# Sums of the tokens added up in DRAM beside S5, a turn without raw copies, and plain products ahead of the sums' products in a hybrid decoder block

## The chip, the cores and the metric

The kernel runs on one core of one Trainium2 chip. The metric is the device time of one execution in microseconds (us). TensorE is called PE, its weight loads PEld, VectorE DVE, ScalarE ACT, GpSimd POOL, and SyncE, which issues most of the loads, SP.

## The reference, cut to what matters

One layer of a decoder block on 1024 tokens of width 1024: a token-mixing sub-layer, a cross-attention into 256 memory rows, and a SwiGLU layer, all in float32. The change lies in the mixing sub-layer:

```python
h = rms_norm(x, g_mix_pre)
z = h @ w_in                                   # 1024 x 4608
z_gm, z_s5, z_ga, z_gb = split(z)              # 2048 | 512 | 1024 | 1024 columns
u, v = split(gelu(z_gm))                       # 2 x 1024
y_gm = u * (W_s (layer_norm(v)) + b_s)         # causal, inside chunks of 128 tokens, 8 groups
y_s5 = s5(z_s5)                                # diagonal complex SSM over all tokens, gelu
y_s5 = y_s5 * sigmoid(y_s5 @ w_glu)
merged = sigmoid(z_ga) * (y_gm @ w_br_gm) + sigmoid(z_gb) * (y_s5 @ w_br_s5)
x = x + rms_norm(merged @ w_mix_out, g_mix_post)
```

## The kernel before, in words

**Products.** Every float32 factor is split into two float32r parts, hi and lo = value - hi (`put`, L527: ACT copies hi, DVE subtracts), and a product is three float32r matmuls (`mm3`, L521). The normed input h stands turned (channels on partitions) in `hT`, eight pairs of 128 x 1024; its first 512 columns are the first half of the tokens (h0), the others the second (h1). `self.slot()` takes one of 38 SBUF tiles of 128 x 1024, `self.bank()` one of the 8 PSUM banks; a new holder waits until the old one's last use.

**Order.** All engines' programs are written out by hand, in one order. The main line writes PE's products; after every six or so it calls `sub()` (L67), a step, which lets each queued generator (`bg`, with a delay in steps) write its next piece and then splits the next weights (`pump`, `split`, L98, with L103 on ACT and L104 on DVE; the weights' loads L94 are on SP, three ahead). `yield n` in a generator means n steps. Each engine works through its own instructions strictly in this order and stops where a semaphore isn't there yet; the DMAs that SP, ACT and POOL issue stand in those queues too.

**Start.** `start` (L650) projects the memory to keys and values and meanwhile turns x: `xgen` squares, scales and, in `h_turn` (L766), transposes four token tiles per k into one bank, from which ACT (L533) and DVE (L140) make the pair in `hT`. For 12 of the 16 banks ACT then also copies the scaled raw value (L783), negated for some, and POOL stores it to `td` in DRAM (L784). Then the S5 parameters are loaded (L203 to L209) and turned (L220).

**S5 and gates.** `s5_in`, `gates` (16 gate blocks, whose results wait in DRAM) and two `u_block`s are the main line, while `s5_gen` (L720) runs eight S5 blocks: `s5_c` rotates and scans on DVE, `s5_d` (L498, with L506 to L508 on PE) gives y, which is turned (L755, copied by ACT at L756) and stored to `yd`.

**u and v.** The remaining u columns (in pairs m = 2, 4, 6) and all v columns use Winograd's form of a 2 x 2 block product: seven products instead of eight, on sums of token blocks (T1 to T4) and sums of weight blocks. `h_split` (L787) makes the token sums behind S5: SP loads the raw parts into slots, POOL adds with accumulating DMAs (L791) from `td` and `hT`, and each sum is split by `put` or by L824; T3, T2 and T4 come each from the sum before, by further adds. `w_ops` (L900) does the weights: `uv_sides` (L926) loads them and names POOL's sums (L137), ACT casts (L912), DVE subtracts; up to eight such operands stand ahead. `u_pairs` (L991) takes them in the order 11, 21, T1, T2, 22, T3 per pair, T4 with the next pair. `v_phase` (L1121) runs 11, T1, T2, 22, T3, 21 and T4 into the banks X (four) and Y (four), with gelus, the layer norm `ln`, and `wturn` (L1193), which transposes W_s (L1198, copied by ACT at L1199), behind T4.

**Gate and gating.** `s5_out` (L1035) makes S5's gate (L1051) and then projects S5's branch (`bs`, evicted by DVE), and from its second weight block on `gm_gen` (L1234) multiplies v with W_s per group and half: PE, two DVE operations (L1257, L1259), and a `put`. `merge` (L1266) needs all eight groups.

```python
        for m in (2, 4, 6):
            prod(b, "11", True)
            prod(e, "21", True)
            prod(d, "T1", True)
            prod(b, "T2", False)
            prod(d, "22", False)
            prod(b, "T3", False)      # T4 with the next pair
```

Of the kernel before, what the change touches and what calls it, by code (L numbers as in the profile page):

```python
# [9 lines left out]
F = mybir.dt.float32  # L10
# [26 lines left out]
class Builder:  # L37
# [565 lines left out]
    def consts(self):  # L603
        nc, i = self.nc, self.ins
        self.ident = self.cp.tile([P, P], F, name="ident", tag="ident")
        make_identity(nc, self.ident)
        g = self.cp.tile([40, P], F, name="grow", tag="grow")
        for j, n in enumerate(("g_mix_pre", "g_ca_pre", "g_ffn_pre", "g_mem", "gm_ln_g")):
            nc.sync.dma_start(g[8 * j:8 * j + 8], i[n][0].rearrange("(k p) -> k p", p=P))
        self.gc = self.cp.tile([P, 48], F, name="gc", tag="gc")  # L610
        ps = self.bank()
        nc.tensor.transpose(ps[:, 0:40], g, self.ident[0:40, 0:40])
        nc.vector.tensor_copy(self.gc[:, 0:40], ps[:, 0:40])
        self.ts(self.gc[:, 40:48], self.gc[:, 0:8], -1.0, ALU.mult)
# [35 lines left out]
    def start(self):  # L650
# [27 lines left out]
        def xgen():  # L678
            for half in range(2):
# [10 lines left out]
                yield from self.h_turn(xs[4 * half:4 * half + 4], half)  # L690
# [4 lines left out]
            self.bg(self.s5_gen(), 5)  # L695
        self.bg(xgen())
# [23 lines left out]
    def s5_gen(self):  # L720
# [28 lines left out]
        for q in range(4):  # L749
            y, t = self.yq.pop(q), self.slot()  # L750
            for jh in range(2):
                ps = self.bank()
                for j in range(4):
                    o = (4 * jh + j) * 128
                    self.nc.tensor.transpose(ps[:, j * 128:j * 128 + 128], y[:, o:o + 128], self.ident)  # L755
                self.nc.scalar.copy(t.rearrange("p (c j) -> p j c", j=8)[:, 4 * jh:4 * jh + 4],  # L756
                                    ps.rearrange("p (j c) -> p j c", j=4))
                yield 2
# [3 lines left out]
            y = t = None  # L762
        yield 1
        self.nc.scalar.dma_start(*late)

    def h_turn(self, xs, half):  # L766

        nc = self.nc
        if not half:
            self.td = self.dr.tile([12, P, 512], F, name="td", tag="td")  # L770
        o = slice(half * 512, half * 512 + 512)
        r = None
        for k in range(8):
            ps = self.bank()
            for t, x in enumerate(xs):
                nc.tensor.transpose(ps[:, t * 128:t * 128 + 128], x[:, k * 128:k * 128 + 128], self.ident)
            self.put_scaled(tuple(z[:, o] for z in self.hT[k]), ps, self.gc[:, k:k + 1])
            if not half or k < 4:
                if k % 2 == 0:
                    r = self.slot()  # L780
                c = slice(k % 2 * 512, k % 2 * 512 + 512)
                n = 40 if half or k >= 4 else 0
                nc.scalar.mul(r[:, c], ps, self.gc[:, n + k:n + k + 1])  # L783
                nc.gpsimd.dma_start(self.td[8 * half + k], r[:, c])  # L784
            yield 1

    def h_split(self):  # L787

        nc = self.nc
        h0, h1 = slice(0, 512), slice(512, 1024)  # L790
        acc = lambda dst, src: nc.gpsimd.dma_start(dst, src, accum_op=ALU.add)  # L791
        raw = [self.slot() for _ in range(4)]
        for k in range(4):
            nc.sync.dma_start(raw[k][:, h0], self.td[8 + k])
            nc.sync.dma_start(raw[k][:, h1], self.td[8 + k])
        for k in range(4):
            acc(raw[k][:, h0], self.td[k])
        for z in range(2):
            for k in range(4):
                acc(raw[k][:, h1], self.hT[k + 4][z][:, h1].bitcast(F))  # L800
            yield 1

        def t1():
            for k in range(4):
                self.put(tuple(x[:, h1] for x in self.hT[k]), raw[k][:, h0])
                if k % 2:
                    yield 1
            self.sides.add("T1")
        early = self.plain
        if early:  # L810
            yield from t1()
        for k in range(4):
            self.put(self.fx("T3", k, True), raw[k][:, h1])
            acc(raw[k][:, h1], self.td[k])
            if k % 2:
                yield 1
        self.sides.add("T3")
        if not early:
            while not self.plain:
                yield 1  # L820
            yield from t1()
        for k in range(4):
            dst, x = self.fx("T2", k, True), raw[k][:, h1]
            nc.scalar.mul(dst[0], x, -1.0)  # L824
            self.stt(dst[1], x, -1.0, dst[0].bitcast(F), ALU.mult, ALU.subtract)
            acc(raw[k][:, h1], self.td[4 + k])
            if k % 2:
                yield 1
        self.sides.add("T2")
        for k in range(4):  # L830
            self.put(self.fx("T4", k, True), raw[k][:, h1])
            if k % 2:
                yield 1
        self.sides.add("T4")
# [91 lines left out]
    def uv_sides(self):  # L926
# [5 lines left out]
        def raw(m):  # L932
            g, u = self.wr.tile([P, 1024], F, name="wr", tag="wr"), self.slot()
            for t, c in ((g, m * 128), (u, m * 128 + 128)):
                ld(t.rearrange("p (k c) -> p k c", k=8), wi[:, c:c + 128].rearrange("(k p) c -> p k c", p=P))
            return g, u
        nxt, old = raw(2), None
        for m in (2, 4, 6):
            g, u = nxt
            nxt = raw(m + 2) if m < 6 else None  # L940
            d, s = self.tmp(), self.tmp()
            yield g[:, h0], ()
            yield g[:, h1], ()
            if old is not None:
                yield old, ()
            yield d, ((d, u[:, h0], u[:, h1], A),)
# [3 lines left out]
            old, g, u = u[:, h1], None, None  # L950
# [6 lines left out]
        r = {}  # L957
        for k in range(2):
            r[k] = row(k)
        for k in (2, 3, 4, 5, 6, 7):  # L960
            r[k] = row(k)
        a, b = [r[k] for k in range(4)], [r[k + 4] for k in range(4)]
        r.clear()
        for k in range(4):
            yield a[k][:, h0], ()
        yield old, ()
# [24 lines left out]
    def u_pairs(self):  # L991
# [14 lines left out]
        fin = None  # L1006
        for m in (2, 4, 6):
            b, d, e = self.bank(), self.bank(), self.bank()
            u, v = self.slot(), self.slot()
# [4 lines left out]
            if fin:  # L1014
                fin()
# [16 lines left out]
            b = d = e = u = v = None  # L1032
        return fin

    def s5_out(self):  # L1035
# [28 lines left out]
        lg(1)  # L1064
        late = []
# [16 lines left out]
        self.bg(self.gm_gen(), 1)  # L1082
# [38 lines left out]
    def v_phase(self, fin):  # L1121
# [71 lines left out]
        def wturn():  # L1193
            for h in (h0, h1):
# [5 lines left out]
                yield 2  # L1200
            for h in (h0, h1):
# [5 lines left out]
                yield 1  # L1207
# [16 lines left out]
        Y = None  # L1224
        run(X, "T4", False)
# [6 lines left out]
        self.bg(wturn(), 3)  # L1232

    def gm_gen(self):  # L1234
# [11 lines left out]
        for g in range(8):  # L1246
# [3 lines left out]
            for half in range(2):  # L1250
# [10 lines left out]
                yield 1 + half  # L1261
# [608 lines left out]
    def go(self, out):  # L1870
        i = self.ins
        self.make_plan()
        self.s5s, self.yq, self.zok, self.xok, self.vok, self.yok, self.plain, self.vhalf = {}, {}, False, False, False, False, False, False
# [7 lines left out]
        self.bg(self.w_ops(self.uv_sides()), 1)  # L1881
# [57 lines left out]
```

## Time and profile before

| | us |
|---|---|
| median of 3 runs | 1700.07 |
| lowest, highest | 1698.69, 1701.0 |
| the profiled execution's own time | 1700.28 |
| its span, first to last instruction | 1698.6 |
| PE busy in the span | 1642.0 |
| DVE, ACT, POOL busy | 1148.9, 688.9, 69.8 |
| granted PE clock, mean | 0.986 |

The granted clock is PE's, as a share of full speed; its two levels are 1.2 and 2.4 GHz, so 0.5 means the lower one. PE's matmuls are pipelined, so durations of neighbours overlap and the distance between starts tells the rate. An idle time stands in brackets behind an instruction, with the instruction or transfer that ended it.

### The profile page before, as it was taken

The page shows a single profiled execution, that of the slowest core. Times are in us where ns is not written, and L with a number is a line of the kernel's source. Part 1 is how long each engine was busy: PE and PEld are TensorE (multiplying, and loading weights), DVE is VectorE, ACT ScalarE, POOL GpSimd, SP SyncE. Part 2 cuts the span into 40 slices and gives each one's busy share as a digit, 9 for nine tenths or more (in the row PEclk, how much of TensorE's full clock was granted, in tenths as well). Part 3 has the DMA queues.
Part 4 walks back from the last instruction along what each step waited for, and adds up shares of the span by engine and source line. Part 5 has one row for each costly group of instructions (what it writes and reads, how often), then busy time and mean ns, then how long its engine had stood idle before and what let it go on. Part 6 is the DMA issues. An engine that isn't in the chain of part 4 may idle for free.

```text
span 1698.6 us, 20955 instructions
## 1 busy us (share of the span) xinstructions
PE 1642.0 (97%) x7788; PEld 1369.9 (81%) x7788; DVE 1148.9 (68%) x2046; ACT 688.9 (41%) x1200; POOL 69.8 (4%) x73
## 2 busy tenths in 40 slices
PE   7899999997999899999999999999999999999998
PEld 7688878875888787888888888888888888888886
DVE  5569788975335476437765567796777778676778
ACT  6622222225446522124554347763333233244454
POOL 0100000034230000000000000000000000000000
PEclk9899999997999999999999999999999999999999
DMA  8532313167440356345431334674544546363634
GB/s 291 183 98 75 95 66 94 58 170 156 149 161 18 122 208 223 124 149 186 149 112 50 126 127 132 208 226 155 183 141 153 186 137 203 134 234 128 226 111 168
DMA packets 206069, 251.13 MB, mean 148 GB/s; under 512 B 14312, under 2 KB 138256, under 8 KB 205968
## 3 DMA queue, kind: packets, MB, share of 16 engines
q1 hardware_dynamic: 175056, 179.14, 33.1%
q10 hardware_dynamic: 26496, 60.18, 9.5%
q0 software_dynamic: 4416, 10.49, 2.6%
q8 instruction: 61, 1.00, 0.2%
q14 instruction: 40, 0.33, 0.1%
HBM read 180.16 MB, written 65.80 MB: 145 GB/s over the span
## 4 chain that ended last, share of the span: by engine, by line
PE 56%; DVE 3%; ACT 1%; issue 1%; DMA 1%; DVEq 0%; ACTq 0%
PE ps L519 55%; DVE act L134 1%; DVE act L140 1%; DMA wr<-actd 1%; DVE ws L134 1%; ACT jk L575 0%; PE ps L1443 0%; PE ps L1397 0%; PE ps L587 0%; DVE ws L104 0%; DVE act L530 0%; DVE st L140 0%; ACT act L529 0%; ACT act L1385 0%; ACT ws L103 0%
## 5 line engine op out<-in xcount | busy, mean ns | idle before, releaser
L519 PE MATMUL ps<-act,ws 128*128 128x512 f32 (+1 forms) x4212 | 975.5, 389 | 15.1 <-ACT act L824 4.2
L519 PEld LDWEIGHTS ps<-act,ws 128*128 128x128 f32 x4212 | 776.4, 189 | 174.6 <-ACT act L824 5.8
L519 PE MATMUL ps<-ws,act 128*128 128x512 f32 x1392 | 339.2, 400 | 4.2 <-ACT ws L103 2.5
L519 PEld LDWEIGHTS ps<-ws,act 128*128 128x128 f32 x1392 | 273.3, 209 | 53.1 <-ACT ws L103 3.4
L134 DVE TENSOR_TENSOR act<-act 128x512 f32<-128x512 f32 (+6 forms) x521 | 290.8, 587 | 15.6 <-ACT act L1051 8.4
L519 PE MATMUL ps<-ws 128*128 128x512 f32 x852 | 193.3, 389 | 0.0
L104 DVE TENSOR_TENSOR ws<-wr,ws 128x1024 fp32r<-128x1024 f32 x100 | 122.0, 1223 | 100.2 <-ACT ws L103 100.2
L519 PEld LDWEIGHTS ps<-ws 128*128 128x128 f32 x852 | 159.9, 188 | 33.2
L134 DVE TENSOR_TENSOR act<-ps,act 128x512 f32<-128x512 f32 x201 | 135.9, 685 | 34.8 <-PE ps L519 32.0
L134 DVE TENSOR_TENSOR ws<-tm,ws 128x512 fp32r<-128x512 f32 x108 | 81.4, 755 | 82.7 <-ACT ws L1522 58.5
L134 DVE TENSOR_TENSOR ws<-act,ws 128x512 fp32r<-128x512 f32 x107 | 73.9, 691 | 89.1 <-ACT ws L1729 51.8
L134 DVE TENSOR_TENSOR ws<-wr,ws 128x512 fp32r<-128x512 f32 x130 | 92.3, 711 | 50.3 <-ACT ws L912 35.2
L1522 ACT CAST ws<-tm 128x512 fp32r<-128x512 f32 x88 | 54.8, 622 | 168.3 <-PE ps L519 115.2
L103 ACT CAST ws<-wr 128x1024 fp32r<-128x1024 f32 x100 | 104.5, 1047 | 43.7 <-PE ps L519 32.5
L529 ACT CAST act<-act 128x512 fp32r<-128x512 f32 (+1 forms) x92 | 57.6, 639 | 124.7 <-DVE act L134 117.2
L530 DVE TENSOR_TENSOR act<-act 128x512 fp32r<-128x512 f32 (+1 forms) x92 | 64.7, 713 | 53.4 <-ACT act L529 47.2
L519 PE MATMUL ps<-act 128*128 128x256 f32 (+2 forms) x504 | 87.3, 319 | 4.2 <-ACT act L1199 4.0
L519 PEld LDWEIGHTS ps<-act 128*128 128x128 f32 x504 | 75.0, 191 | 14.4 <-ACT act L1199 4.9
L1729 ACT CAST ws<-act 128x512 fp32r<-128x512 f32 x71 | 44.2, 622 | 89.6 <-PE ps L519 48.3
L530 DVE TENSOR_TENSOR act<-ps,act 128x512 fp32r<-128x512 f32 x48 | 32.5, 688 | 39.7 <-ACT act L529 39.7
L877 ACT ACTIVATE act<-ps 128x512 f32<-128x512 f32 x32 | 19.2, 601 | 77.6 <-PE ps L519 50.8
L1806 POOL DMA_DIRECT2D out_dram<-act x4 | 2.2, 554 | 1170.5 <-DVE act L134 1170.5
(164 smaller groups left out, 1080.1 us busy)
## 6 DMA issues: line engine op xcount, KB each, us to landing
wr<-in_ffn_w_gu_dram SPq DMA_DIRECT2D x39, 512.0 KB, 4.1
actd<-act ACTq DMA_DIRECT2D x77, 256.0 KB, 2.1
wr<-actd SPq DMA_DIRECT2D x38, 512.0 KB, 3.6
wr<-in_w_in_dram SPq DMA_DIRECT2D x28, 512.0 KB, 3.9
act<-in_ffn_w_gu_dram SPq DMA_DIRECT2D x22, 512.0 KB, 5.1
act<-in_ffn_w_down_dram SPq DMA_DIRECT2D x44, 256.0 KB, 4.4
pd<-act ACTq DMA_DIRECT2D x17, 512.0 KB, 3.7
act<-pd SPq DMA_DIRECT2D x34, 256.0 KB, 4.3
```

Source lines behind the costliest of these rows:

```text
L103: self.nc.scalar.copy(hi, t)
L104: self.nc.vector.tensor_tensor(out=lo, in0=t, in1=hi.bitcast(F), op=ALU.subtract)
L134: self.nc.vector.tensor_tensor(out=out, in0=a, in1=b, op=op)
L140: self.nc.vector.scalar_tensor_tensor(out=out, in0=a, scalar=s, in1=b, op0=op0, op1=op1)
L519: self.nc.tensor.matmul(ps, a, b, start=start, stop=stop, skip_group_check=more)
L529: self.nc.scalar.copy(dst[0], src)
L530: self.nc.vector.tensor_tensor(out=dst[1], in0=src, in1=dst[0].bitcast(F), op=ALU.subtract)
L877: nc.scalar.activation(out=g[:, half * 512:half * 512 + 512], in_=ps, func=AF.Sigmoid)
L1522: self.nc.scalar.copy(t[:, 0:512], now)
L1729: nc.scalar.copy(w[:, h[0]], src)
L1806: nc.gpsimd.dma_start(out[t * P:t * P + P], os_[t])
```

## The change

x's turn becomes the plain `turn` and makes only the pairs in `hT`. A new generator `h_sums` starts eight steps after x is turned and makes T1 to T4 in a DRAM tile `td` of 20 parts of 128 x 512: ACT negates the two parts of h that are subtracted, and POOL stores, copies and adds with DMAs from `hT` and from `td` itself. `h_split` loads each finished sum on SP and splits it, T2 ahead of T1 while the u blocks still read `hT`, T3 and T4 not before y is turned. y's turn is copied by DVE, one step apart instead of two, and S5's last product comes one step later. The weights' operands start five steps later and in a new order, since the plain products (11 and 21) of pairs 2 and 4 now come first and those of pair 6 behind pair 4; fewer rows of the v weights are loaded at once. `wturn` starts ahead of T4's run, with longer distances, and `gm_gen` three steps into the first block of S5's branch, two steps between halves.

```diff
                 yield 4
-                yield from self.h_turn(xs[4 * half:4 * half + 4], half)
+                yield from self.turn(xs[4 * half:4 * half + 4], 0, hs(half))
                 for t in range(4):
                     xs[4 * half + t] = None
             self.xok = True
             self.s5_load()
             self.bg(self.s5_gen(), 5)
+            self.bg(self.h_sums(), 8)
...
             if b < 7:
                 yield from self.s5_b(b + 1)
             else:
-                yield 3
+                yield 4
             yield from self.s5_d(b)
...
-                self.nc.scalar.copy(t.rearrange("p (c j) -> p j c", j=8)[:, 4 * jh:4 * jh + 4],
-                                    ps.rearrange("p (j c) -> p j c", j=4))
-                yield 2
+                self.nc.vector.tensor_copy(t.rearrange("p (c j) -> p j c", j=8)[:, 4 * jh:4 * jh + 4],
+                                           ps.rearrange("p (j c) -> p j c", j=4))
+                yield 1
...
+        self.yturned = True
...
-    def h_turn(self, xs, half):
...
+    def h_sums(self):
...
+        self.td = self.dr.tile([20, P, 512], F, name="td", tag="td")
+        part = lambda j, k: self.td[4 * j + k]
+        add = lambda dst, src: nc.gpsimd.dma_start(dst, src, accum_op=ALU.add, max_dma_last_dim=512)
+        self.T = {"T1": 0, "T3": 1, "T2": 2, "T4": 3}
+        for j, (o, h) in ((0, (0, h1)), (4, (4, h0))):
+            for k in range(4):
+                n = self.slot()
+                for c, z in ((h0, 0), (h1, 1)):
+                    nc.scalar.mul(n[:, c], self.hT[k + o][z][:, h].bitcast(F), -1.0)
+                nc.gpsimd.dma_start(part(j, k), n[:, h0])
+                yield 2
+                add(part(j, k), n[:, h1])
+                yield 2
+                n = None
+        for k in range(4):
+            nc.gpsimd.dma_start(part(1, k), part(0, k))
+        yield 4
+        for j, o, h in ((1, 4, h1), (0, 0, h0)):
+            for z in range(2):
+                for k in range(4):
+                    add(part(j, k), self.hT[k + o][z][:, h].bitcast(F))
+                    yield 1
+                yield 4
+        for k in range(4):
+            nc.gpsimd.dma_start(part(2, k), part(1, k))
+            yield 1
+        yield 4
+        for z in range(2):
+            for k in range(4):
+                add(part(2, k), self.hT[k][z][:, h0].bitcast(F))
+                yield 1
+            yield 4
+        for k in range(4):
+            nc.gpsimd.dma_start(part(3, k), part(2, k))
+            yield 1
+        yield 4
+        for k in range(4):
+            add(part(3, k), part(4, k))
+            yield 1
...
     def h_split(self):
...
+        def ld(n):
+            r = []
             for k in range(4):
+                if k % 2 == 0:
+                    r.append(self.slot())
+                nc.sync.dma_start(r[-1][:, k % 2 * 512:k % 2 * 512 + 512], self.td[4 * self.T[n] + k])
+            return r
+        raw = {n: ld(n) for n in ("T1", "T2")}
+        todo = ["T1", "T2", "T3", "T4"]
+        while todo:
+            n = todo[todo[0] == "T1" and not self.plain and len(todo) > 1]
+            while n == "T1" and not self.plain:
+                yield 1
+            todo.remove(n)
+            if n not in raw:
+                raw[n] = ld(n)
+            r = raw.pop(n)
+            while n in ("T3", "T4") and not self.yturned:
+                yield 1
+            for k in range(4):
+                x = r[k // 2][:, k % 2 * 512:k % 2 * 512 + 512]
+                if n == "T1":
+                    self.put(tuple(z[:, 512:1024] for z in self.hT[k]), x)
+                elif n == "T2":
+                    dst = self.fx(n, k, True)
+                    nc.scalar.mul(dst[0], x, -1.0)
+                    self.stt(dst[1], x, -1.0, dst[0].bitcast(F), ALU.mult, ALU.subtract)
+                else:
+                    self.put(self.fx(n, k, True), x)
                 if k % 2:
                     yield 1
...
+            self.sides.add(n)
...
+        gs = [raw(m) for m in (2, 4, 6)]
+        us = [raw(3)]
+        for g in gs[:2]:
             yield g[:, h0], ()
             yield g[:, h1], ()
...
+            if j == 1:
+                yield gs[2][:, h0], ()
+                yield gs[2][:, h1], ()
...
+        a, b = [row(k) for k in range(4)], []
         for k in range(4):
             yield a[k][:, h0], ()
+            b.append(row(k + 4))
...
+        plain(2)
+        plain(4)
+        fin = lambda: None
+        for m in (2, 4, 6):
+            b, d = bank.pop(m), self.bank()
+            u, v = out.pop(m), self.slot()
             prod(d, "T1", True)
             nc.scalar.copy(v[:, h1], d)
+            fin()
             prod(b, "T2", False)
             nc.scalar.copy(u[:, h1], b)
+            self.later()
             prod(d, "22", False)
...
+            if m == 4:
+                plain(6)
...
         lg(1)
+        self.bg(self.gm_gen(), 3)
         late = []
         w = self.get(("bs", 0))
...
-        self.bg(self.gm_gen(), 1)
...
                 nc.scalar.copy(self.wt[:, h], ps)
-                yield 2
+                yield 4
...
                 self.tt(self.bb[:, h], ps, self.bb[:, h], ALU.add)
-                yield 1
+                yield 2
...
         Y = None
+        self.bg(wturn(), 2)
         run(X, "T4", False)
...
         self.bg(ln(0))
-        self.bg(wturn(), 3)
...
                 self.put(tuple(s[:, o] for s in y), u[:, o])
-                yield 1 + half
+                yield 2
...
-        self.bg(self.w_ops(self.uv_sides()), 1)
+        self.bg(self.w_ops(self.uv_sides()), 6)
```

## Rows read from the trace of the kernel before

**Rows 1.** Stretches: PE, PEld, DVE, ACT, POOL busy (instructions), granted clock, DMA share, GB/s.
```profile
43.13:111.23 68.10, 58.20 (x231) 48.35 (x229) 41.46 (x132) 30.70 (x46) 6.71 (x11) 0.90 0.50 159
361.29:363.89 2.60, 2.60 (x26) 2.60 (x24) 0.00 (x0) 0.00 (x0) 0.00 (x0) 1.00 0.29 65
378.49:431.15 52.66, 39.23 (x156) 30.13 (x155) 27.64 (x41) 26.67 (x40) 21.63 (x22) 0.77 0.70 139
82.00:355.00 273.00, 267.18 (x1397) 229.34 (x1398) 225.95 (x569) 64.44 (x118) 3.97 (x4) 0.99 0.29 87
546.19:578.69 32.50, 28.00 (x127) 22.49 (x126) 14.20 (x30) 25.03 (x44) 0.00 (x0) 0.95 0.16 51
```
**Rows 2.** The same view for the products of L519 alone (PE, PEld).
```profile
43.13:111.23 68.10, 55.16 (x192) 44.17 (x192) 0.90 0.50 159
378.49:431.15 52.66, 31.78 (x100) 20.91 (x100) 0.77 0.70 139
```
**Rows 3.** Timeline of PE, start: start, duration, instruction, count, [idle before, what ended it].
```profile
52.70 0.50 PE L519 MATMUL ps<-ws,act 128*128 128x512 f32 x1 [1.64 <-ACT ws L103]
53.96 10.20 PE L519 MATMUL ps<-ws,act 128*128 128x512 f32 x29 [0.76 <-DVE ws L104]
65.68 0.30 PE L776 MATMUL ps<-ident,act 128*128 128x128 f32 x1 [1.52 <-DVE act L144]
...
92.73 0.22 PE L220 MATMUL ps<-ident,act 32*128 32x32 f32 x1 [3.25 <-DMA act<-in_s_lam_re_dram]
...
93.35 17.95 PE L519 MATMUL ps<-ws,act 128*128 128x512 f32 x66
```
**Rows 4.** Timeline of ACT in the first turn: a raw copy and a split of weights.
```profile
48.94 0.69 ACT L783 ACTIVATE act<-ps,gc 128x512 f32<-128x512 f32 x1 [1.36 <-DVE act L140]
...
51.61 1.03 ACT L103 CAST ws<-wr 128x1024 fp32r<-128x1024 f32 x1
```
**Rows 5.** Timeline of PE from S5's last block to the first u pair.
```profile
378.49 0.38 PE L506 MATMUL ps<-act 128*128 128x128 f32 x2
...
388.09 4.36 PE L519 MATMUL ps<-act,ws 128*128 128x512 f32 x18
...
406.32 0.79 PE L519 MATMUL ps<-act,ws 128*128 128x512 f32 x1 [3.83 <-ACT act L824]
...
423.80 2.93 PE L519 MATMUL ps<-act,ws 128*128 128x512 f32 x9 [3.20 <-ACT act L1019]
```
**Rows 6.** Timeline of ACT, DVE and POOL in the same stretch.
```profile
365.12 0.62 ACT L912 CAST ws<-wr 128x512 fp32r<-128x512 f32 x1 [7.94 <-DMA act<-act]
...
371.39 4.87 DVE L134 TENSOR_TENSOR act<-act 128x512 f32<-128x512 f32 x3
...
376.84 4.92 POOL L791 DMA_DIRECT2D act<-act  x4
...
390.09 0.87 POOL L791 DMA_DIRECT2D act<-act  x1 [0.40 <-DMA act<-act]
...
420.71 1.08 ACT L756 COPY act<-ps 128x512 f32<-128x512 f32 x1 [5.13 <-DVE act L530]
```
**Rows 7.** Timeline of PE and DVE from v's products to S5's gate.
```profile
480.91 65.44 PE L519 MATMUL ps<-ws,act 128*128 128x512 f32 x288
540.67 2.48 DVE L134 TENSOR_TENSOR act<-ps,act 128x512 f32<-128x512 f32 x4
...
560.85 1.16 PE L519 MATMUL ps<-act 128*128 128x128 f32 x8 [4.02 <-ACT act L1199]
```
**Rows 8.** DVE by line, 590 to 650: count, busy us, mean ns, idle before, releaser.
```profile
L530 DVE TENSOR_TENSOR act<-act 128x512 fp32r<-128x512 f32 x16 | 11.1, 693 | 11.1 <-ACT act L529 11.1
L134 DVE TENSOR_TENSOR act<-tm,act 128x512 f32<-128x512 f32 x16 | 11.1, 692 | 4.3 <-DMA act<-ud 3.8
```
**Rows 9.** Timeline of PE where the merge begins.
```profile
646.27 0.49 PE L519 MATMUL ps<-act,ws 128*128 128x512 f32 x1 [3.14 <-ACT act L529]
```

More of the change, by code (lines that the diff above doesn't have):

```diff
@@ L609, in consts @@
             nc.sync.dma_start(g[8 * j:8 * j + 8], i[n][0].rearrange("(k p) -> k p", p=P))
-        self.gc = self.cp.tile([P, 48], F, name="gc", tag="gc")
+        self.gc = self.cp.tile([P, 40], F, name="gc", tag="gc")
         ps = self.bank()
         nc.tensor.transpose(ps[:, 0:40], g, self.ident[0:40, 0:40])
-        nc.vector.tensor_copy(self.gc[:, 0:40], ps[:, 0:40])
-        self.ts(self.gc[:, 40:48], self.gc[:, 0:8], -1.0, ALU.mult)
+        nc.vector.tensor_copy(self.gc, ps[:, 0:40])
     def make_plan(self):
@@ L762, in s5_gen @@
             y = t = None
+        self.yturned = True
         yield 1
         self.nc.scalar.dma_start(*late)
-    def h_turn(self, xs, half):
+    def h_sums(self):
         nc = self.nc
[L769 to L784, printed above, removed]
+        h0, h1 = slice(0, 512), slice(512, 1024)
+        self.td = self.dr.tile([20, P, 512], F, name="td", tag="td")
[36 more added lines that the diff above has]
+            add(part(3, k), part(4, k))
@@ L789, in h_split @@
         nc = self.nc
[L790 to L798, printed above, removed]
-            for k in range(4):
-                acc(raw[k][:, h1], self.hT[k + 4][z][:, h1].bitcast(F))
-            yield 1
@@ L806, in t1 @@
                 if k % 2:
                     yield 1
[L808 to L834, printed above, removed]
+            r = None
+            self.sides.add(n)
     def hx(self, name, k):
@@ L932, in raw @@
         def raw(m):
[L933 to L941, printed above, removed]
+            t = self.wr.tile([P, 1024], F, name="wr", tag="wr") if m % 2 == 0 else self.slot()
+            ld(t.rearrange("p (k c) -> p k c", k=8), wi[:, m * 128:m * 128 + 128].rearrange("(k p) c -> p k c", p=P))
+            return t
+        gs = [raw(m) for m in (2, 4, 6)]
+        us = [raw(3)]
+        for g in gs[:2]:
             yield g[:, h0], ()
             yield g[:, h1], ()
+        old = None
+        for j in range(3):
+            g, u = gs[j], us.pop()
+            if j < 2:
+                us.append(raw(2 * j + 5))
+            d, s = self.tmp(), self.tmp()
+            yield d, ((d, u[:, h0], u[:, h1], A),)
             if old is not None:
                 yield old, ()
-            yield d, ((d, u[:, h0], u[:, h1], A),)
             yield s, ((s, d, g[:, h0], A),)
@@ L1005, in prod, with plain @@
             self.sub()
[L1006 to L1009, printed above, removed]
+        bank = {}
+        out = {}
+        def plain(m):
+            b, e = self.bank(), self.bank()
+            bank[m] = b
+            u = out[m] = self.slot()
             prod(b, "11", True)
@@ L1872, in go @@
         self.make_plan()
-        self.s5s, self.yq, self.zok, self.xok, self.vok, self.yok, self.plain, self.vhalf = {}, {}, False, False, False, False, False, False
+        self.s5s, self.yq, self.zok, self.xok, self.vok, self.yok, self.plain, self.vhalf, self.yturned = {}, {}, False, False, False, False, False, False, False
         self.fxs, self.ops, self.late, self.yT, self.sides = {}, [], [], [], {"11", "21", "22"}
```

16 lines of the change are left out of this document (2 added, 14 removed).

## The prediction

> **What bounds the kernel now.** I read the busy shares by stretches first: a gain can come only from where TensorE (PE) waits or runs at a lower clock. Two stretches stand out. From 43.13 to 111.23 us the granted clock is 0.90 and PE is busy 58.20 of 68.10 us; from 378.49 to 431.15 it is 0.77, with 39.23 of 52.66 [rows 1]. Counting the products in them [rows 2] and pricing each at the undisturbed rate tells what they ought to take: 288 products in 65.44 us are 0.227 us each [rows 7].
>
> Start: 192 products are 43.6, eight groups of four 128-column transposes as much as eight products more (1.8), the S5 parameters' small ones about 1: 46.5 of 68.1 us. **21.5 us are lost.** Handover from S5 and the gates to the u pairs: 100 products 22.7, eight groups of transposes 1.8, S5's last products 2.6 (an earlier block's took 361.29 to 363.89) [rows 1]: 27.1 of 52.7. **25.5 us are lost.** Smaller places are 4.02 us at S5's gate [rows 7] and 3.14 us where the merge begins [rows 9]. In S5's own stretch (82 to 355) PE is busy 267 of 273 us, DVE 226, ACT 64, POOL 4, the DMA engines 29% [rows 1]: all but PE and DVE have room there.
>
> **Part 1, x's turn without raw copies (h_turn, L766, becomes turn, L582).** Removed: 12 ACT copies of 0.69 us and 12 POOL stores. The copies cost more than 12 x 0.69 = 8.3 us: each waits for DVE's subtraction from the same bank (1.36 us in the row shown), and the split of the next weights (L103, 1.03 us) stands behind it on ACT [rows 4]. PE needs that split: 1.64 us at 52.70, 0.76 for DVE's half of it, and then 29 products in 10.20 us where 6.6 would do [rows 3]. From 43.13 to 64.16 there are 54 products, 12.3 us of work in 21.0: 8.7 lost, and ACT's queue is the reason. Without the copy ACT has 0.69 per turn step and half a split, 1.2 us, against six products and a group of transposes (1.6) on PE, so it keeps up, and I take all 8.7 as gained. What is late next: the second half of x is squared by ACT and scaled by DVE before its turn (65.68, waiting for DVE L144) [rows 3]; PE comes 8.7 us sooner, the squares do not keep that pace, so I gain 1 of that place's 3. After it the S5 parameters' load (3.25 us at 92.73, then 66 products in 17.95 where 15.0 would do) [rows 3] stands on SP behind the weights' loads, which wait for the same splits; earlier splits move it, but PE is earlier as well: 2 of 6. Sum 11.7; bounds 4 (if the arrival of the weights takes over from ACT) and 17.
>
> **Part 2, the sums in DRAM beside S5 (h_sums).** Added: 16 ACT multiplies (at 0.69, 11 us over some 32 steps of six products, 1.4 us each; ACT has the room) and 56 POOL DMAs of 256 KB: 8 stores, 36 accumulating adds, 12 DRAM copies. The yields spread them over about 112 steps, some 157 us, from about 80 to 240. POOL's only other work there is two memsets for S5's first block, which have 80 us. Issuing a DMA takes POOL 0.87 us alone and 1.23 beside DVE [rows 6]: 49 to 69 us. No row shows an add in DRAM. The nearest are the adds into SBUF, the last of them 1.28 us apart with each waiting for an earlier one [rows 6]; in DRAM I take between that and twice that, 72 to 144 us of the DMA engines' time in a stretch that leaves 70% of them free. S5's chain on DVE sees none of it. I charge 1 us, bounds 0 and 6 (weights' loads or S5's small DMAs late).
> The Trainium skill (DMA: Bandwidth & Descriptors, Anatomy of one DMA) gives such a DMA about 2.0 us fixed plus bytes over 436 GB/s, and calls HBM the target that is slowest to confirm a write; an estimate by it is 2.6 us each, 146 us if all 56 ran one behind the other, and the charge would stay as it is.
>
> **Part 3, the handover.** (a) S5's last block: 2.6 us of PE work take from 378.49 to 388.09, 7.0 lost [rows 5]. DVE was late: w_ops' first cast stood 7.94 us on ACT behind S5's eight small DMAs, DVE's subtraction waited for that cast and S5's rotation stood behind the subtraction; then three of DVE's products took 4.87 us beside POOL's sums [rows 6]. The delay of w_ops by five steps puts S5's rotation ahead of the casts, and `yield 4` gives DVE one step (1.4 us) more. Gain 5.5, leaving 1.5 for POOL's sums that still meet the rotation. (b) The waits for T2 (3.83 and pieces after it) and for the bank's copy (3.20), with the lower clock behind them, are the other 18.5 [rows 5]. T1 and T2 now lie summed in DRAM by about 240, SP's eight loads wait for slots alone, and four plain products (4 x 12 x 0.227 = 10.9 us) stand ahead of T1 in place of two. T4 no longer takes y's slot before y's turn is done, the tangle in which ACT's y copy waited 5.13 us [rows 6]. What is late next is DVE: y's eight copies are now its own (1.08 on ACT [rows 6]; 0.7 to 1.2 here), with eight subtractions for T1 and T2, eight for the weights and four for T3 at 0.69 [rows 8]: 20 to 24 us, where PE has 12 steps of 1.36 and the transposes, 18 us. T3 is due some six steps after its puts, so I leave 4 us of waits: 14.5 gained. Sum of part 3: 20; bounds 8 and 25.
>
> **Part 4, S5's gate and the gating.** Turning W_s during T4 instead of behind it removes the 4.02 us but asks for a PSUM bank while all eight hold X and Y. By the rate above T4 starts at 535.4 and the turn comes 12 products later, at 538.2; Y's first eviction on DVE begins at 540.67 and takes 0.62 [rows 7]: PE waits about 3.1 us there, new. I hold that neither decides: from 546 to 579 ACT is busy 25.03 of 32.50 us [rows 1], the rest being short waits inside the gate's chain from sigmoid to put, and PE waits for that chain. 0 (bounds -3 and +4). gm_gen starts some 5 us earlier, but behind it DVE has no gap to give: 16 subtractions with 11.1 us of waiting for ACT's casts among them, and 3.8 us for the first u [rows 8]. That u is now asked for ahead of two of the gate loads and lands at most those 3.8 us earlier; in exchange four evictions (2.7 us) queue behind it on DVE. +1 (bounds -2 and +5) of the merge's 3.14 [rows 9] and the lower clock behind it.
>
> **Sum.** 11.7 - 1 + 20 + 0 + 1 = 31.7, taken as 31. The profiled execution took 1700.28 us (span 1698.6, 1.7 around it), 0.2 above the median of the runs: 1700.1 - 31 = **1669**.
>
> **Rivals.**
> *DVE takes over the handover* (18%). For: 20 to 24 us in 18 as above, with POOL's sums to slow it. Against: DVE was busy 27.64 of 52.66 us there [rows 1], and T1 and T2 come early in its order. Half of part 3 is lost: 21 gained, 1679.
> *The start stays as it is* (9%): with ACT free, the weights' DMA or the second half of x bounds it. For: the DMA engines' share is 0.50 over that stretch [rows 1], with nothing to spare in its first part if the loads bunch. Against: the waits name ACT's split [rows 3]. 2 in place of 11.7: 1679.
> *The gate's new bank wait adds up* (9%): if ACT's backlog doesn't hide it, 3.1 us, about 2 at the lower clock behind it and DVE's four evictions cost 6: 1675.
> *Slower: the adds in DRAM still run when their sums are due* (5%). POOL takes its instructions in order, so w_ops' sums stand behind the whole chain, T1's and T2's loads behind its end. From about 85 to about 350 there are 265 us for 56 DMAs: up to 4.7 us each, one behind the other, nothing is lost; at 5.3 the 31 us are used up, and at 5.4 the kernel takes 1705. For: every add waits for the one before it on its part. Against: four parts are in flight at a time, and adds into SBUF were 1.28 apart [rows 6].
> The Trainium skill (SBUF — State Buffer, Who interferes with whom) lets a DVE copy in a two-port mode lock GpSimd out of writing descriptors, and elsewhere on the page a GpSimd DMA of 620 ns took some 3100 ns beside one. Four issues beside DVE's products and scans took 1.23 us each here [rows 6], so the trace doesn't show that lock; by the page's 3.1 us the issues would come to an estimated 174 us, and the chance of this rival would be some 10%.
> *The change doesn't do what it says* (4%): T1's and T2's loads wait for slots until S5's tiles are free, so that T2 is no earlier and 12 of part 3's 20 fail; 1681, and nothing is gained if the start stays too.
>
> **How the numbers follow.** Forecast 55%, the rivals 18, 9, 9, 5 and 4. Below, parts 1 and 3 at their bounds and 5 from the gate would be 1653, which needs everything at once; I take 1657. Above, the cases at 1679 and 1681 lie within, with 7 to 9 us more lost: 1688. A measurement of this kernel can tell about 0.2%, 3.4 us, from no change. Faster by more: 0.91; within it 0.03; slower 0.06, the adds and a little for several failures together.
>
> **What would show it.** Right: no raw copy and no POOL store in the turn, and PE at 0.227 per product from the kv products to the second turn; POOL's adds over by about 260; no PE wait at T2; S5's last products in 3 to 4 us; a new PE wait of about 3 us in T4 at the turn of W_s. Wrong: POOL's DMAs past 340; PE waiting for DVE between the y transposes; PE or ACT waiting for weights from DRAM near 50; S5's blocks longer than before.

## The result and the profile after

The changed kernel takes 1670.49 us (median of 4 runs, 1668.45 to 1672.85); the kernel before, run beside it, 1700.19 (1698.69 to 1701.0). The ratio is 0.9827 [0.981, 0.9844], 29.7 us less. The forecast of 1669 is 1.5 us from it. The profiled execution took 1670.15 us with a span of 1668.4, 30.2 less than the span before. Four marks in PE's timeline divide it: the first S5 parameter turn at L353 (after the one at L220), the start of S5's last block, v's first product, and the first product of the merge.

| stretch | before | after | gained | predicted |
|---|---|---|---|---|
| to S5's first parameter turn | 111.23 | 95.45 | 15.8 | 11.7 |
| from there to S5's last block | 267.26 | 273.19 | -5.9, of which 1.4 is the added step | -1 |
| S5's last block to v's first product | 88.82 | 67.11 | 21.7, of which 1.4 is that step's work | 20 |
| v's first product to the merge | 178.96 | 179.58 | -0.6 | +1 |
| the merge to the end of the span | 1052.33 | 1053.07 | -0.7 | 0 |

So the total is right and the split is not: 4 us more at the start pay for the 4.6 us that S5's stretch lost, where 1 was charged. That the forecast came within 1.5 us is in part luck.

The start, PE's timeline (start, duration, instruction, count, idle before and what ended it), beside [rows 3]:
```profile
42.92 12.52 PE L519 MATMUL ps<-ws,act 128*128 128x512 f32 x54
...
78.14 0.22 PE L220 MATMUL ps<-ident,act 32*128 32x32 f32 x1 [0.46 <-DMA act<-in_s_lam_re_dram]
...
78.86 16.66 PE L519 MATMUL ps<-ws,act 128*128 128x512 f32 x66
95.45 1.09 PE L353 MATMUL ps<-ident,act 32*64 32x32 f32 x16
```
No wait for ACT's split is left; 54 products stand in one row. The load that PE awaited 3.25 us now costs 0.46.

By stretches (PE, PEld, DVE, ACT, POOL busy, granted clock, DMA share, GB/s), beside [rows 1], the start, S5 while the adds run and behind them, and the handover:
```profile
42.92:95.45 52.53, 50.95 (x230) 45.27 (x228) 37.98 (x119) 25.04 (x37) 3.92 (x4) 1.00 0.62 177
140.00:200.00 60.00, 60.00 (x315) 49.86 (x314) 45.30 (x90) 13.70 (x20) 36.42 (x34) 1.00 1.25 228
200.00:220.00 20.00, 15.13 (x81) 12.50 (x80) 19.66 (x35) 1.78 (x3) 3.04 (x3) 0.87 0.69 137
368.64:435.75 67.11, 64.89 (x309) 52.99 (x308) 43.30 (x58) 34.65 (x59) 22.32 (x16) 1.00 0.50 180
```
The handover runs at full clock and PE lacks 2.2 us of it. The new loss is the second and third row: a DMA share above 1 from 140 to 200, and PE 4.9 us idle at a clock of 0.87 just behind. ACT, DVE and PE in that place, first in the kernel before, then in the changed one:
```profile
199.49 5.10 ACTq L453 DMA_DIRECT2D act<-act  x8
207.34 1.22 DVE L104 TENSOR_TENSOR ws<-wr,ws 128x1024 fp32r<-128x1024 f32 x1 [7.89 <-ACT ws L103]
228.86 0.49 PE L508 MATMUL ps<-act 128*128 128x128 f32 x2 [1.43 <-DVE act L134]
```
```profile
184.08 8.73 ACTq L453 DMA_DIRECT2D act<-act  x8
194.34 1.06 ACT L103 CAST ws<-wr 128x1024 fp32r<-128x1024 f32 x1
...
195.43 1.23 DVE L104 TENSOR_TENSOR ws<-wr,ws 128x1024 fp32r<-128x1024 f32 x1 [11.38 <-ACT ws L103]
196.57 11.39 DVE L134 TENSOR_TENSOR act<-act 128x512 f32<-128x512 f32 x15
...
214.99 0.80 PE L507 MATMUL ps<-act 128*128 128x128 f32 x2 [3.75 <-DVE act L134]
216.90 0.80 PE L508 MATMUL ps<-act 128*128 128x128 f32 x2 [1.12 <-DVE act L134]
```
DVE's next 15 products for S5 wait behind a weights' subtraction, that behind ACT's cast, and the cast behind eight small S5 transfers whose issue takes 8.73 us, against 5.10 in the kernel before (and 5.15 here at the block at 246.81, when the adds are over). PE's waits in S5's stretch come to 4.87 us, against 2.33 before (1.43 and another of 0.90 at 256.27). The rest of the 4.6, some 2 us, are products at the lower clock behind them: the granted clock is 0.90 from 210.86 to 245.07.

From the handover on, PE's timeline beside [rows 5], [rows 7] and [rows 9]:
```profile
368.64 0.38 PE L506 MATMUL ps<-act 128*128 128x128 f32 x2
...
371.56 5.04 PE L519 MATMUL ps<-act,ws 128*128 128x512 f32 x21
...
390.04 5.68 PE L519 MATMUL ps<-act,ws 128*128 128x512 f32 x24 [0.65 <-DVE act L134]
397.13 38.78 PE L519 MATMUL ps<-act,ws 128*128 128x512 f32 x168 [1.41 <-ACT act L1038]
...
509.94 0.63 PE L1223 MATMUL ps<-ident,act 128*128 128x128 f32 x4 [3.30 <-DVE act L134]
...
547.75 0.50 PE L519 MATMUL ps<-act,ws 128*128 128x512 f32 x1 [3.56 <-ACT act L529]
...
615.33 45.01 PE L519 MATMUL ps<-act,ws 128*128 128x512 f32 x185 [3.69 <-ACT act L529]
```
S5's last block takes 2.9 us (368.64 to 371.56), no wait for T2 is left, and the bank wait at W_s's turn is there with 3.30 us.

### The profile page after: what moved, and what is told of

It reads as the page before. It is cut to its first block, busy times and chain, and to the rows that moved or that the text cites. A ratio compares the mean times of both kernels' runs of the same rounds, so it can differ in the third digit from the quotient of the medians.

```text
span 1668.4 us, 20995 instructions
## 1 busy us (share of the span) xinstructions
PE 1628.1 (98%) x7788; PEld 1364.4 (82%) x7788; DVE 1150.6 (69%) x2053; ACT 681.7 (41%) x1196; POOL 102.7 (6%) x97
## 4 chain that ended last, share of the span: by engine, by line
PE 83%; DVE 7%; ACT 5%; issue 2%; DMA 2%; SPq 0%; ACTq 0%; DVEq 0%
PE ps L519 79%; DVE act L134 2%; DVE ws L104 1%; ACT jk L575 1%; DVE ws L134 1%; ACT ws L103 1%; DMA wr<-in_ca_w_kv_dram 1%; ACT act L529 1%; DVE act L530 1%; DVE act L140 1%; PE ps L587 1%; ACT jk L1160 1%; DMA wr<-actd 1%; PE ps L508 1%; ACT act L1167 0%
## 5 line engine op out<-in xcount | busy, mean ns | idle before, releaser
L519 PE MATMUL ps<-act,ws 128*128 128x512 f32 (+1 forms) x4212 | 970.1, 388 | 9.6 <-ACT act L529 7.3
L519 PEld LDWEIGHTS ps<-act,ws 128*128 128x128 f32 x4212 | 775.4, 189 | 165.9 <-ACT act L529 8.1
L519 PE MATMUL ps<-ws,act 128*128 128x512 f32 x1392 | 332.8, 395 | 0.0
L519 PEld LDWEIGHTS ps<-ws,act 128*128 128x128 f32 x1392 | 270.2, 208 | 45.0
L134 DVE TENSOR_TENSOR act<-act 128x512 f32<-128x512 f32 (+6 forms) x521 | 287.3, 580 | 15.2 <-ACT act L1076 8.0
L519 PE MATMUL ps<-ws 128*128 128x512 f32 x852 | 193.3, 389 | 0.0
L519 PEld LDWEIGHTS ps<-ws 128*128 128x128 f32 x852 | 159.9, 188 | 33.2
L104 DVE TENSOR_TENSOR ws<-wr,ws 128x1024 fp32r<-128x1024 f32 x100 | 122.1, 1223 | 93.3 <-ACT ws L103 93.1
L519 PE MATMUL ps<-act 128*128 128x256 f32 (+2 forms) x504 | 86.6, 317 | 0.2
L519 PEld LDWEIGHTS ps<-act 128*128 128x128 f32 x504 | 74.7, 190 | 9.6 <-DVE act L134 0.8
```

Of the source, the lines that this page charges most:

```text
L104: self.nc.vector.tensor_tensor(out=lo, in0=t, in1=hi.bitcast(F), op=ALU.subtract)
L134: self.nc.vector.tensor_tensor(out=out, in0=a, in1=b, op=op)
L519: self.nc.tensor.matmul(ps, a, b, start=start, stop=stop, skip_group_check=more)
```

## The experiments

The theory: the start was held by ACT's queue (the copies, not the stores), the handover by late sums and late S5 work, part 4 decides nothing; the adds cost S5 its 4.6 us by crowding the DMA engines. Each run is judged by its own stretches as well as its time, since the start alone differs by up to 4.8 us between profiles of kernels that are equal there (95.45 and 100.20 for the first parameter turn).

**The copies and the stores back (e1_copies_stores), the copies alone (e2_copies_only).**
The second line is in the first run only.
```diff
+                        nc.scalar.mul(r[:, c], ps, self.gc[:, k:k + 1])
+                        nc.gpsimd.dma_start(tx[8 * half + k], r[:, c])
```


> The changed kernel with one part put back: in x's turn each of the twelve banks is copied raw by ACT again and stored by POOL (to a DRAM tile that nobody reads). If ACT's queue was what held the kv products (the prediction's part 1, with 15.6 us seen at the start between the two traces), S5's first parameter turn moves back from 95.5 to 107-112 us, the waits for ACT's split of the weights return near 52 us, and the kernel takes 1682-1687. If the gain at the start has another source (the h_sums' arrival, the order of loads, the start's luck), it stays at 1670-1673.

> As the run before, but ACT's raw copies alone come back, without POOL's stores. ACT's queue as the cause: nearly the whole loss is there without a store, 1680-1686. The stores as the cause (their DMA traffic beside the weights' loads, or banks and slots that they hold): 1670-1673, and the parameter turn at 95-97 us.

Measured: 1686.89 us, 0.9914 [0.9899, 0.9928], and 1685.84, 0.9905 [0.989, 0.992]. PE with the copies alone:
```profile
51.79 0.50 PE L519 MATMUL ps<-ws,act 128*128 128x512 f32 x1 [1.60 <-ACT ws L103]
53.05 2.79 PE L519 MATMUL ps<-ws,act 128*128 128x512 f32 x11 [0.76 <-DVE ws L104]
...
92.02 0.21 PE L220 MATMUL ps<-ident,act 32*128 32x32 f32 x1 [4.76 <-DMA act<-in_s_lam_re_dram]
...
93.00 17.75 PE L519 MATMUL ps<-ws,act 128*128 128x512 f32 x66
```
The parameter turn stands at 110.68 (110.91 with the stores). So 12 ACT copies of a bank cost 15.2 us; the 0.2 for the stores is less than such profiles differ by. The copies also bring the wait for S5's parameters back, 4.76 us, though no transfer was added: the loads on SP stand behind loads of weights whose buffers come free when the weights are split. From 30 to 95 us those loads wait 45.6 us in all for DVE's half of the split (L104) instead of 30.5, and the first load of S5's parameters is issued at 85.17 instead of 71.75.

**The pauses doubled (e3_spread).** So for every pause behind the negations:
```diff
-                    yield 1
-                yield 4
+                    yield 2
+                yield 8
```


> The changed kernel with the pauses between the DRAM copies and adds doubled, so that POOL's chain ends near 300 us in place of 204. Theory A, the adds crowd the DMA engines and S5's eight small transfers per block land late, which costs the 4.6 us by which S5's stretch is longer than before: at half the rate the DMA share of 140-200 us falls from about 1.2 to 0.7, the eight issues on ACT take 5 to 6 us in place of 7.6 and 8.7, PE's 3.8 us wait near 205 us goes, 1665-1668. Theory B, the loss comes from the work of ACT and DVE that the change moved forward (negations, splits of weights), whatever the rate of the adds: 1670-1671 as now. A third outcome: more of S5's blocks are met at a lower rate each, and the loss stays with another place.

Measured: 1672.2 us, 0.9827 [0.9812, 0.9841]; S5's stretch 272.12. It doesn't tell the theories apart, because the edit spread next to nothing: a pause sets only where POOL's instruction stands in program order, and POOL, with nothing else to do, ran on. The chain but its last four adds was issued by 208 us, nearly as before; those four had fallen behind w_ops' sums and ran from 372 to 382:
```profile
207.42 0.49 POOL L804 DMA_DIRECT2D td<-td  x1 [2.75 <-DMA td<-act]
354.72 1.29 POOL L137 TENSOR_TENSOR tm<-act 128x512 f32<-128x512 f32 x1 [146.81 <-DMA act<-in_w_in_dram]
...
381.73 1.00 POOL L773 DMA_DIRECT2D td<-td  x1
```

**The old order of the u pairs (e4_one_pair).** One pair's 11 and 21 products at the head of each pass, and the sides in that order.
```diff
-        plain(2)
-        plain(4)
...
+            prod(b, "11", True)
+            nc.scalar.copy(u[:, h0], b)
+            prod(e, "21", True)
+            self.tt(u[:, h0], e, u[:, h0], ALU.add)
```


> The changed kernel with the old order of the u pairs (one pair's two plain products ahead of T1 instead of two pairs' four, the weights' sides in the old order and started five steps earlier, as before); the sums are still made early. If the early sums carry the handover's 20 us and the order only a little: DVE's list is the same and T1 is needed 5 us earlier, T1 and T3 come 2 to 6 us late, 1672-1677. If the order carries it: 10 or more of the 20 us come back as waits near 390 us, 1680 or more. If the order is worth nothing: 1669-1671.

(The sides still started at the changed kernel's step, not earlier as stated above.) Measured: 1675.56 us, 0.9845 [0.9825, 0.9864]. PE waits 3.61 us where T1's puts are due (and 0.71 near 402 for T3's):
```profile
384.20 0.50 PE L519 MATMUL ps<-act,ws 128*128 128x512 f32 x1 [0.74 <-ACT act L529]
386.86 2.04 PE L519 MATMUL ps<-act,ws 128*128 128x512 f32 x6 [2.16 <-DVE act L530]
389.61 1.22 PE L519 MATMUL ps<-act,ws 128*128 128x512 f32 x2 [0.71 <-DVE act L530]
```
From S5's last block to W_s's turn it takes 146.50 us against 141.30: the order is worth 5.2. No run undid the early sums alone.

**S5's tail as before (e5_tail).**
```diff
-                yield 4
+                yield 3
...
-        self.bg(self.w_ops(self.uv_sides()), 6)
+        self.bg(self.w_ops(self.uv_sides()), 1)
```


> The changed kernel with S5's tail as before: w_ops asked for one step ahead instead of six, and a pause of three steps instead of four ahead of S5's last products. If the delay is what freed S5's last block (the prediction's part 3a): w_ops' cast stands behind the eight small transfers again, DVE's rotation behind it, S5's last block takes 7 to 10 us in place of 2.9, and the kernel 1673-1677 after 1.4 us less of the pause. If it was the absence of POOL's sums and early put work alone: the block stays under 4 us and the kernel at 1668-1671.

Measured: 1677.84 us, 0.9861 [0.9845, 0.9877]. ACT, DVE and PE:
```profile
354.45 0.62 ACT L925 CAST ws<-wr 128x512 fp32r<-128x512 f32 x1 [7.96 <-issue]
...
355.10 0.69 DVE L134 TENSOR_TENSOR ws<-wr,ws 128x512 fp32r<-128x512 f32 x1 [5.85 <-ACT ws L925]
...
369.45 0.49 PE L507 MATMUL ps<-act 128*128 128x128 f32 x2 [1.24 <-DVE act L134]
372.44 0.80 PE L508 MATMUL ps<-act 128*128 128x128 f32 x2 [2.50 <-DVE act L134]
```
The cast waits 7.96 us behind S5's issues as it did before [rows 6], S5's last block takes 8.9 us (367.83 to 376.73) in place of 2.9: 6.0 for the two small edits, with the DRAM adds long over. Which of the two carries it no run tells.

**The adds left out (e14_noadds), the adds paced by the gates (e13_paced), half of S5's issues on SP (e16_sp).** The edits in this order; the POOL sum of the second stands ahead of the groups of copies and adds.
```diff
-        add = lambda dst, src: nc.gpsimd.dma_start(dst, src, accum_op=ALU.add, max_dma_last_dim=512)
+        add = lambda dst, src: None
...
+                self.gt(pt, self.last, self.last, ALU.add)
...
-            nc.scalar.dma_start(tv[16 * k:16 * k + 16, :, 16 * k:128], kv[:, :, 0:128 - 16 * k])
+            (nc.sync if k % 2 else nc.scalar).dma_start(tv[16 * k:16 * k + 16, :, 16 * k:128], kv[:, :, 0:128 - 16 * k])
```


> The changed kernel without the 36 adds (the stores and DRAM copies stay, so the sums and what is made of them are wrong). It prices the adds: theory A, S5's stretch from the first parameter turn to the last block loses its 4.6 us and the wait near 205 us is at most the 1.4 us of before, 1664-1666; theory B, 1669-1671. Nothing else may move, as the handover's loads waited for no add.

> The run with doubled pauses left the adds where they were, since nothing on POOL waits for the pauses. Here POOL also adds four columns of the gate half tile just made to themselves before each group of DRAM copies and adds, so that it must wait for the gates; pauses doubled. The chain should then end near 300 us. Theory A (the adds crowd the DMA engines, and S5's small transfers land late): DMA share under 0.9 in each 20 us, the eight issues of a block on ACT at 5.1 to 6 us, no PE wait over 1.5 us in 200-220, and 1665-1667. Theory B (work of ACT and DVE that moved forward in S5's first blocks, whatever the adds): the 3.8 us wait stays, 1670.

> The changed kernel with four of the eight small transfers of each S5 block asked for by SP instead of ACT; the adds stay where they are. The theory after the run without adds: DVE takes its work in order, S5's next block stands behind the subtraction of a weights' split, this waits for ACT's cast, and the cast stands behind the eight issues; the adds stretch the issues from 5.1 us to 7.6 and 8.7, and DVE's wait from 7.8 to 11.4. With half of the issues on SP the cast comes 2.5 to 4.4 us sooner, PE's waits of 3.8 and 1.1 us shrink to 2 together or less, and S5's stretch from the first parameter turn to the last block falls from 273.2 to 268-270; with the start as in the changed kernel 1665-1668. Rival: the adds reach PE by another way (the small transfers land late, SP's loads of weights stand behind the issues that wait for DVE), and the stretch stays at 272 or grows.

Measured: 1669.85 us, 0.9814 [0.98, 0.9829]; 1669.97, 0.9815 [0.98, 0.983]; 1666.37, 0.9791 [0.9776, 0.9807]. The first two look like theory B by their times alone, but their profiles had a start 4 us longer. With the paced adds this lies ahead of everything that the edit touches. Without the adds it does not quite: the first add would have stood at 79 us, 3.3 of the 4.2 us arise behind that, where PE waits 1.34 and 0.89 us for S5's parameters, and all four runs took 1669.0 to 1670.7. So it can't be excluded that this edit has a part in it. S5's stretch tells: without the adds 268.57 us, 4.6 less than with them, all that it had lost. ACT, DVE and PE of that run, then SP, ACT and DVE of the one that shares the issues:
```profile
187.98 5.09 ACTq L453 DMA_DIRECT2D act<-act  x8
195.76 1.23 DVE L104 TENSOR_TENSOR ws<-wr,ws 128x1024 fp32r<-128x1024 f32 x1 [7.81 <-ACT ws L103]
217.27 0.49 PE L508 MATMUL ps<-act 128*128 128x128 f32 x2 [1.43 <-DVE act L134]
```
```profile
184.31 3.63 SPq L453 DMA_DIRECT2D act<-act  x4
184.31 3.48 ACTq L453 DMA_DIRECT2D act<-act  x4
190.82 1.23 DVE L104 TENSOR_TENSOR ws<-wr,ws 128x1024 fp32r<-128x1024 f32 x1 [6.54 <-ACT ws L103]
```
DVE's wait at that one subtraction goes with S5's stretch through the kernels (the kernel before with its missing step of 1.37 added):

| kernel | DVE's wait for the cast | S5's stretch |
|---|---|---|
| shared issues (e16) | 6.54 | 266.2 |
| no adds (e14) | 7.81 | 268.6 |
| before | 7.89 | 268.6 |
| adds paced by the gates (e13) | 8.98 | 270.1 |
| pauses doubled (e3) | 10.01 | 272.1 |
| changed | 11.38 | 273.2 |

The other eight lie close to the same line (5.50 and 265.2 for e19, 13.02 and 274.4 for e8).

The adds reach PE by this one chain: slow issue on ACT, a late cast, DVE behind it. Late landing of the small transfers, the other half of theory A, is not the way: at this block they landed 5.8 us after their issue in the median, against 2.6 without the adds, but 7.0 in e16, where the adds were still there (DMA share 1.22 from 140 to 200) and the loss was gone with the shorter issue. That the adds lengthen the issue is shown. That they do so by crowding the engines is argued from the DMA share, 1.37 during the eight issues and 0.16 without the adds. Crowding is not all: in e13 the issue took 6.28 us at a share of 0.14, since one transfer took 1.79 to issue with no add under way, and why stays open. The paced adds gained 3.1 us in S5's stretch, but their last four fell behind w_ops' sums again (374 to 385).

**Part 4 undone (e18_part4).** The old pauses in both generators as well.
```diff
-        self.bg(wturn(), 2)
...
         self.bg(ln(0))
+        self.bg(wturn(), 3)
...
-        self.bg(self.gm_gen(), 3)
...
         lg(2)
+        self.bg(self.gm_gen(), 1)
```


> The changed kernel with the prediction's part 4 undone: W_s turned behind T4 as before, the gating's queue started after the third gate load with its old pauses. By the prediction's reading neither decides: the 3.3 us wait in T4 goes, a wait of 2 to 4 us stands in S5's gate again, the stretches from v's products to the gate products and from there to the merge stay within 1.5 us of the changed kernel's, and the kernel at 1669-1672. Rivals: the bank wait in T4 is a true loss, 1667; or the earlier turn and gating gave their 3 to 4 us and other places lost as much, 1673-1675.

Measured: 1671.63 us, 0.9821 [0.9808, 0.9834]. The bank wait goes and the gate's wait comes back:
```profile
530.94 2.08 PE L519 MATMUL ps<-act 128*128 128x128 f32 x8 [3.99 <-ACT act L1224]
...
616.19 43.97 PE L519 MATMUL ps<-act,ws 128*128 128x512 f32 x180 [3.15 <-ACT act L529]
```
From v's first product (437.40) to the merge 178.79 us, against 179.58: part 4 moves one wait of 3 to 4 us to another place and gains nothing that these runs can tell.

**The gating's subtraction a half tile later (e8_lo).**
```diff
-                self.put(tuple(s[:, o] for s in y), u[:, o])
+                self.nc.scalar.copy(y[0][:, o], u[:, o])
+                if lo:
+                    self.tt(*lo, ALU.subtract)
+                lo = y[1][:, o], u[:, o], y[0][:, o].bitcast(F)
...
+        self.tt(*lo, ALU.subtract)
```


> The changed kernel with the gating's subtraction (the low half of each gated tile) put one half tile later on DVE, so that DVE doesn't wait for ACT's cast. If DVE's waits for the casts bound the gating (11 us of waits over 16 half tiles), the 3.7 us wait at the merge and its lower clock go: 1664-1667. If the gating follows its own steps and the wait at the merge is the chain behind the last half tile alone: 1669-1671, the wait about 3 us as now.

Measured: 1664.59 us, 0.9784 [0.977, 0.9799]. PE has no wait at the merge:
```profile
608.25 51.94 PE L519 MATMUL ps<-act,ws 128*128 128x512 f32 x228
```
From the gating's last products to the end of the span it takes 1055.45 us against 1062.58, 7.1 less: the wait of 3.69, and 2.9 for the 185 products behind it, which ran at 0.243 us each in the changed kernel (granted clock 0.94 from 615.33 to 660) and at 0.228 here (1.00).

**Both together (e17_best), and paced as well (e19_best_paced).** No new edit but longer pauses between the groups in the second.


> The changed kernel with the subtraction of the gating put a half tile later (1664.6 alone, 0.9784 of the kernel before) and half of S5's small issues on SP. If the two gains lie in different stretches and add up: 7 us from the first and 3 to 5 from the second, 1659-1662. If they share the same slack, or SP's issues hold up loads: 1664-1666.

> As the run before, with the adds paced by the gates too (a POOL sum of four columns of each new gate half tile ahead of the next group), pauses doubled between the groups only, so that the chain ends near 260-290 us. If the crowding still costs something once the issues are shared: 1 to 2 us less than the run before. If the shared issues hide it: the same within 1.5 us.

Measured: 1659.02 us, 0.9749 [0.9735, 0.9762], and 1658.99, 0.975 [0.9737, 0.9763]. The gains add up: of the kernel before's time, 0.43% by e8 and 0.36% by e16 beyond the changed kernel, 0.78% together, some 13 us. Pacing shortens S5's stretch further (265.15 against 267.42, with no PE wait there at all), yet the time is the same: in the profiles its start was 1.2 us longer, and from S5's gate to the gating's last products it took 57.86 us against 56.54, a difference whose cause stays open.

## Why the prediction held, and where it did not

**Start, 11.7 predicted, 15.8 found.** The mechanism was right, and the copies alone carry it. The 8.7 for the kv products came out as 8.7 (their stretch ends at 55.28 in place of 64.16, begun 0.2 earlier). The two terms that I had discounted were mis-sized: the second half of x gave 2.9 where I left 1, the parameters' load and the 66 products behind it 4.0 where I left 2. My argument for the discount, that PE comes earlier too, forgot that the squares and the loads stand in the same queues and come earlier with it: the second turn began at 55.28 in place of 65.68, the parameters' turn at L220 at 78.14 in place of 92.73. These are also the uncertain terms: in the profiles of e13 and e14 the turn stood at 100.20 and 99.70, with 66 products in 18.08 and 17.94 us, and a gain of some 11. Small slips in the sums carry no weight: a group of four transposes takes 0.35 us (58.66 to 59.01) where I priced 0.23, the terms of the start add up to 46.4, the adds' rival at 5.4 us each comes to 1706, and the two failures named with 1681 would together still leave 9 us of gain.

**S5, 1 charged, 4.6 found.** This step failed, inside its bounds of 0 and 6. The engines' time was bounded well: POOL's 56 DMAs took 68.1% of the 16 engines from 74 to 210 us, 92.6 us, inside 72 to 144 (this is the sum of their packets' times, which overlap: the share went above 1). They ended at 205, not 240, since the yields spread nothing on POOL, as e3 shows. The sentence that fell is "S5's chain on DVE sees none of it". The chain had been read already, in part 3: a cast stood 7.94 us behind S5's eight issues on ACT [rows 6], and DVE behind the cast. In the kernel before DVE waited so at earlier blocks too, 7.89 us at 207, 5.80 at 238 and 3.87 at 266, and I priced it only at the last. One of the signs named for being wrong, S5's blocks longer than before, was there.

**Handover, 20 predicted, 20.3 found.** (a) 5.5 for the tail, 6.0 by e5. (b) 14.5 for the rest; the order gives 5.2 of it, which leaves some 9 for the early sums and what came with them (y's copies on DVE, T4's slot), not told apart by a run. Of the 4 us of waits that I left for DVE 2.1 came, and only 0.65 of them ended with DVE; the other 1.41 ended with ACT's copy of a bank. The rival that DVE takes over did not come; with the order undone PE's waits are for the puts of T1 and T3, most of them ended by DVE, and it costs the 5.2.

**Part 4, 0 and +1 predicted, -0.6 in all.** The bank wait of 3.1 was 3.30, and neither the new wait nor the old one decides, as e18 shows. The gating gained nothing, since DVE's waits for ACT's casts bound it; e8 shows what was to be had there, 7.1 us.

The rival of the adds that run too late is out: the last was issued at 204.44, some 147 us before SP's first load of a sum (352.08) and the first of w_ops' sums on POOL (354.93). The Trainium skill (SBUF — State Buffer, Who interferes with whom) lets a DVE operation in a two-port mode that issues first block GpSimd for its whole length. This trace shows no lock of some 3 us for each: the 32 adds with a source in SBUF took 1.32 us to issue in the median and 3.64 at most.

## What to carry to other kernels

A background transfer is not free because its engines have room on average: find which in-order queue issues small transfers beside it, and what stands behind that queue; a cast behind eight issues on ACT cost 4.6 us more here, and sharing the issues with another queue gained 7 in that stretch. When a copy is taken from a queue, price all that stands behind it, the loads whose buffers that queue frees included. A pause in program order paces nothing on an engine that has no other work; only a wait does.

## What the runs showed of the hardware

An add of 256 KB into DRAM took far more of the DMA engines than a copy: with the adds the packets of POOL's queue took 92.6 us of all 16 engines from 74 to 210 us, without them 11.3% or 15.4 us for 20 stores and copies (0.77 us each), so 2.14 us for each of the 36 adds. Two things differ, though. The change asks for the adds in pieces (`max_dma_last_dim=512`), and each went out as 528 packets (20017 in that window with the adds, 1024 without). Twelve adds of the same size into SBUF in the kernel before had 144 packets each and took 1.48 us each (1728 packets, 59.3% of 370 to 400 us). How much of the price is the adding in DRAM and how much the small packets, no run tells; the same adds without the pieces are the experiment that is missing here.

With the adds under way, ACT needed 8.73 us to issue eight transfers that took 5.09 without them, and in e8 10.37; issue is not a fixed price. And behind a single PE wait of 3.69 us the products took 2.9 us more at the lower clock (0.94 granted, against 1.00 in e8).
